# Down projection: each chunk begins with products of the first half of the tokens; layernorm's reciprocals written ahead of the gate evictions that follow

## Chip, cores, metric

One core of a Trainium2 chip runs the whole layer. The metric is the time of one execution on the device in microseconds (us), the median over runs of the same program. TensorE (PE) multiplies, VectorE (DVE) and ScalarE (ACT) do elementwise work and copy results out of PSUM, GpSimd (POOL) and SyncE (SP) here only issue transfers (DMA).

## The reference, cut to what matters

All tensors are float32; SEQ and D_MODEL are 1024, D_FF is 2816, D_CONF and D_SC 512, PLE_DIM 256, one layer.

```
h = rmsnorm(x, g_mix)
z = h @ w_in        # columns: conformer value | gate | shortconv B | C | V | merge gates A | B
a = a_val * sigmoid(a_gt)
a = causal_dwconv(a, conv_a_w) + conv_a_b                  # width 31
a = silu(layernorm(a, ln_a_g, ln_a_b))
y_a = a @ w_a_out
s = sc_b * causal_dwconv(sc_c * sc_v, conv_b_w)            # width 3
y_b = s @ w_b_out
x = x + (g_a * y_a + g_b * y_b) @ w_o
h = rmsnorm(x, g_ffn)
u = h @ w_up                                               # 1024 x 5632
f_gate = causal_dwconv(u[..., :D_FF], conv_f_w) + conv_f_b # width 3
f = gelu(f_gate) * u[..., D_FF:]
x = x + f @ w_down                                         # 2816 x 1024
x = x + sigmoid(rmsnorm(x, g_ple) @ w_ple_gate) * (p @ w_ple)
return rmsnorm(x, g_final)
```

## The kernel before, in words

Everything lies transposed: channels on the 128 partitions, the 1024 tokens along the free axis, in two halves H0 and H1 of 512 columns. One row is a tile of 128 channels x 1024 tokens. A float32 product is made of three products of rounded parts: each operand is cut into a hi (a cast on ScalarE, line 132) and a lo (a subtraction on VectorE, line 133), and hi by hi, lo by hi and hi by lo are added up in PSUM.

The input, up and down projections multiply two row blocks by two column blocks of weights with seven instead of eight products (Strassen in Winograd's form). The class Pair does one pair of output rows. Its method step(m) runs product m, of 3 matmuls for each input row pair: 1 and 2 multiply the two halves of the plain weights w_r by plain first-half columns of the rows, product 1 being copied to a second bank (line 639); 6 and 7 multiply sums of weights (s12 and s34, split into w_s_hi and w_s_lo) by sums of rows and go on in the copied bank, and after each of them the bank is copied out as u (lines 646 and 652); 5 is a sum by a sum too, 4 takes the plain weights w_q, 3 a sum of weights and plain columns. Its results go to four methods: use11 (after product 2), use21 (after 4), sum12 (after 3) and sum22 (after 5 and 7), the last two being the second half of the tokens. Of each pair of input rows four sums of quarters are needed (tiles t in the trace; fs is the split of those for products 5 and 7, ft of those for 6 and 4), and three plain quarters, f_q, for products 1, 2 and 3.

TensorE and SyncE work in the order in which the code is written. The order of ScalarE, VectorE and POOL is set by a scheduler while the program is built; tc.keep_in_program_order marks an instruction whose written place the scheduler is to keep against those written before it. On the chip each engine then works strictly along its own list, and an instruction that waits holds up all behind it.

The down projection takes its 22 rows of f, as 11 pairs, in three chunks of 4, 4 and 3 pairs (DROWS). Each chunk runs four pairs of output rows (p from 0 to 3) in the order that block_order makes: (0,1), (1,1), (0,2), (1,2), then (0,6), (0,5), (0,7) and so on, where (p, m) is product m of pair p. A product has 12 matmuls in the first two chunks and 9 in the last. Four products stand ahead of the first product 6. The rows of f were stored to HBM by the up projection; the class Rows loads them (load: two rows of 512 KB each), splits the plain quarters (plain) and makes and splits the sums (sums). Method prepare(ci, left) calls these by the products left in the work before. For the first chunk the rows are loaded six and three products before the up projection's end and the sums made at its last products; for the others loads stand 14 products ahead, plain splits 5, sums 2, 1 and 0.

In the first two chunks DnStore takes the results: it fills two tiles dn of 128x1024 and, once both halves are there, POOL adds each to x1 in HBM with an accumulating DMA of 512 KB (line 1152). In the last chunk DnLast loads the rows of x1 (both rows of the pair at its product 1), adds to them on VectorE (lines 1190 to 1201) and splits the result for the product with w_ple_gate. The class Loader fetches weights on SyncE's queue; the sums of weights are made by accumulating DMAs on POOL's queue (line 244).

The layernorm: ln_end runs between the products of s with w_b (gate evictions on line 922 are `gate = ps * gate`): variances by two small matmuls, sqrt on ScalarE, two reciprocals of 128x512 on VectorE (line 387, lrstd), then acc times lrstd (line 912), silu and the split to an_hi and an_lo, which TensorE needs for the products with w_a.

## Time and profile before

| what | value |
|---|---|
| runs shown: median (lowest, highest) | 1379.69 us (1376.6, 1381.29), 3 runs |
| profiled execution, its time | 1382.37 us |
| its span in the profile | 1380.6 us |
| TensorE busy | 1306.8 us (95%), 5798 matmuls |
| VectorE, ScalarE, POOL busy | 976.6 (71%), 590.3 (43%), 247.1 us (18%) |
| DMA | 245.25 MB, mean 178 GB/s |
| first matmul of the down projection's chunks | 1023.68, about 1117.6, about 1206.7 us |
| down projection ends | 1272.75 us |

The profile is of one execution, and its durations are read against its own span; the median of the runs is 2.7 us below this execution. Busy time of TensorE counts matmuls at half clock as busy too, so 95% doesn't mean that 5% is all that can be had. In a timeline a line says when an instruction began, how long it took and, in brackets, how long its engine had been idle and what ended that.

### The profile page before, as it was taken

The numbers are of one execution on the slowest core, as the hardware profiler recorded it, in microseconds if no ns is written. First come the engines' busy times: TensorE is split into PE (matmuls) and PEld (weight loads), VectorE is DVE, ScalarE is ACT, GpSimd is POOL, SyncE is SP. The second block draws the span as 40 slices with busy tenths as digits, with TensorE's granted clock in tenths as the row PEclk, the third lists the DMA queues.
The fourth block names the chain that finished last, engine by engine and source line by source line (L and its number), as shares of the span: only waits on it lengthen the run. The fifth ranks groups of instructions, "written<-read, shape, count | busy, mean of one in ns | idle before, by whom it ended". The sixth has DMA issues, their size and how long they took to land.

```text
span 1380.6 us, 15699 instructions
## 1 busy us (share of the span) xinstructions
PE 1306.8 (95%) x5798; PEld 1081.9 (78%) x5798; DVE 976.6 (71%) x1134; ACT 590.3 (43%) x814; POOL 247.1 (18%) x319
## 2 busy tenths in 40 slices
...
GB/s 339 183 119 125 179 237 159 142 200 212 196 272 233 122 24 130 163 205 189 177 167 175 198 186 172 174 168 192 187 181 162 272 222 204 211 234 153 76 91 73
DMA packets 102765, 245.25 MB, mean 178 GB/s; under 512 B 11680, under 2 KB 21664, under 8 KB 102688
## 3 DMA queue, kind: packets, MB, share of 16 engines
...
## 4 chain that ended last, share of the span: by engine, by line
PE 71%; DVE 14%; issue 8%; DMA 3%; ACT 2%; POOL 1%; SPq 0%; DVEq 0%; ACTq 0%; POOLq 0%
PE ps L629 50%; PE ps L155 14%; DVE acc L712 2%; PE ps L969 2%; PE ps L968 2%; PE ps L970 2%; DMA x_d<-dn 2%; DVE w_s_lo L133 1%; POOL s L244 1%; DMA f<-f_d 1%; DVE w_r_lo L133 1%; DVE x_raw L477 1%; DVE ft_lo L133 1%; DVE sc_cv L712 1%; DVE t L588 1%
## 5 line engine op out<-in xcount | busy, mean ns | idle before, releaser
L712 DVE SCALAR_TENSOR_TENSOR acc<-a,prm,acc 128x1023 f32<-128x1023 f32 (+14 forms) x120 | 151.8, 1265 | 1.7
L133 DVE TENSOR_TENSOR w_s_lo<-s,w_s_hi 128x1024 fp32r<-128x1024 f32 (+1 forms) x100 | 119.6, 1198 | 35.7 <-ACT w_s_hi L132 35.7
L244 POOL DMA_DIRECT2D s<-s x100 | 85.6, 856 | 298.2 <-DMA s<-s 126.0
L652 ACT COPY u<-ps 128x512 f32<-128x512 f32 x50 | 29.3, 586 | 202.3 <-PE ps L629 202.3
L132 ACT CAST w_s_hi<-s 128x1024 fp32r<-128x1024 f32 (+1 forms) x100 | 102.9, 1031 | 2.6 <-issue 1.7
L712 DVE SCALAR_TENSOR_TENSOR fg<-u_t,neg_f,fg 128x1023 f32<-128x1023 f32 (+1 forms) x44 | 56.5, 1283 | 28.3 <-ACT fg L706 27.6
L133 DVE TENSOR_TENSOR w_r_lo<-raw_r,w_r_hi 128x1024 fp32r<-128x1024 f32 (+1 forms) x50 | 59.8, 1197 | 17.2 <-ACT w_r_hi L132 17.2
L646 ACT COPY u<-ps 128x512 f32<-128x512 f32 x50 | 29.3, 586 | 92.4 <-PE ps L629 92.4
L629 PE MATMUL ps<-xgs_hi,w_s_lo 128*128 128x512 f32 x176 | 68.6, 390 | 0.0
L629 PE MATMUL ps<-xgs_lo,w_s_hi 128*128 128x512 f32 x176 | 68.5, 389 | 0.0
L629 PE MATMUL ps<-xgs_hi,w_s_hi 128*128 128x512 f32 x176 | 68.5, 389 | 0.0
L629 PE MATMUL ps<-xgp_hi,w_r_lo 128*128 128x512 f32 x176 | 68.5, 389 | 0.0
L629 PE MATMUL ps<-xgp_lo,w_r_hi 128*128 128x512 f32 x176 | 68.5, 389 | 0.0
L629 PE MATMUL ps<-xgp_hi,w_r_hi 128*128 128x512 f32 x176 | 68.5, 389 | 0.0
L639 ACT COPY ps<-ps 128x512 f32<-128x512 f32 x50 | 28.5, 571 | 87.6 <-PE ps L629 87.6
L1075 DVE TENSOR_TENSOR u_t<-ps,rstd 128x512 f32<-128x512 f32 x22 | 15.2, 691 | 69.7 <-PE ps L629 69.7
L155 PE MATMUL ps<-xp_hi,whi 128*128 128x448 f32 (+2 forms) x192 | 62.0, 323 | 1.9 <-DVE x L1201 1.9
L629 PE MATMUL ps<-xgq,w_s_hi 128*128 128x512 f32 x176 | 55.8, 399 | 7.2 <-DVE u_t L665 7.2
L155 PE MATMUL ps<-xp_lo,whi 128*128 128x448 f32 (+2 forms) x192 | 61.9, 323 | 0.0
L155 PE MATMUL ps<-xp_hi,wlo 128*128 128x448 f32 (+2 forms) x192 | 61.9, 323 | 0.0
L629 PE MATMUL ps<-xgt_hi,w_q 128*128 128x512 f32 x176 | 57.9, 390 | 0.7 <-ACT u L652 0.7
L629 PE MATMUL ps<-hss_hi,w_s_hi 128*128 128x512 f32 x128 | 50.9, 398 | 4.5 <-ACT w_s_hi L132 4.5
...
## 6 DMA issues: line engine op xcount, KB each, us to landing
s<-s POOLq DMA_DIRECT2D x92, 256.0 KB, 4.1
raw_r<-w_up SPq DMA_DIRECT2D x22, 512.0 KB, 4.7
s<-w_up SPq DMA_DIRECT2D x44, 256.0 KB, 3.0
s<-w_up SPq DMA_DIRECT2D x22, 512.0 KB, 5.8
s<-w_up POOLq DMA_DIRECT2D x44, 256.0 KB, 6.0
f_d<-v_t POOLq DMA_DIRECT2D x22, 512.0 KB, 5.9
f<-f_d SPq DMA_DIRECT2D x22, 512.0 KB, 9.8
s<-w_in SPq DMA_DIRECT2D x32, 256.0 KB, 3.2
```

The lines of the kernel that those rows point to most:

```text
L132: nc.scalar.copy(hi, src)
L133: nc.vector.tensor_sub(lo, src, f32(hi))
L155: nc.tensor.matmul(ps[:, :step], wt[:, b], xt[:, t : t + step], start=f, stop=l)
L244: nc.gpsimd.dma_start(dst, src, accum_op=ALU.add)
L629: nc.tensor.matmul(ps, wt[:, b], xt, start=f, stop=l, skip_group_check=True)
L639: nc.scalar.copy(self.b, self.a)
L646: nc.scalar.copy(self.e[:, H0], self.b)
L652: nc.scalar.copy(self.e[:, H1], self.b)
L712: nc.vector.scalar_tensor_tensor(dst[:, s:], src[:, : T - s], w(k), dst[:, s:], ALU.mult, ALU.add)
L968: nc.tensor.matmul(ps, whi[:, b], hi, start=first and k == ks[0], stop=False)
L969: nc.tensor.matmul(ps, whi[:, b], lo, start=False, stop=False)
L970: nc.tensor.matmul(ps, wlo[:, b], hi, start=False, stop=last and k == ks[-1])
```

## The change

In the down projection dn_order replaces block_order. In the first chunk all four products 1 come first, then all four products 2; in the other two they are interleaved as (0,1), (1,1), (0,2), (2,1), (1,2), (3,1), (2,2), (3,2). So eight products stand ahead of the first product 6, all of which need plain quarters of the first half of the tokens alone. In the rest of the chunk product 4 of a pair stands behind product 6 of the next. The last chunk ends with (3,4), (3,5), (3,3), where before it ended with (3,5), (3,4), (3,3).

Rows are loaded by halves: load0 the first-half tokens of a pair's two rows, load1 the second-half ones, as two DMAs of 256 KB each. The table STEPS gives, for the first chunk and for the others, the product at which each step of each pair of rows is written: negative numbers count back from the chunk's begin, positive ones from its first product. Sums are made in place and split in pairs (split23, split14). DnStore stores each half as soon as it is there: accumulating DMAs of 128x512, 256 KB, twice as many. DnLast loads the second row of its pair at product 6 and not at product 1.

In the layernorm, ln_end is cut in two. ln_stats has the variances, sqrt and reciprocals, and the first gate eviction of that round (first half) is marked to keep its written place, behind the reciprocals; the rest of ln_end is written behind the evictions of the round.

```diff
         return ap.bitcast(F32)
-    def halve(hi, lo, src):
-        nc.scalar.copy(hi, src)
+    def halve(hi, lo, src, pinned=False):
+        ins = nc.scalar.copy(hi, src)
+        if pinned:
+            tc.keep_in_program_order(ins)
         nc.vector.tensor_sub(lo, src, f32(hi))
...
         return order + [(n - 1, 4), (n - 1, 3)]
+    def dn_order(ci):
+        if ci == 0:
+            order = [(p, m) for m in (1, 2) for p in range(4)]
+        else:
+            order = [(0, 1), (1, 1), (0, 2), (2, 1), (1, 2), (3, 1), (2, 2), (3, 2)]
+        order += [(0, 6), (0, 5), (0, 7)]
+        for p in (1, 2):
+            order += [(p, 6), (p - 1, 4), (p, 5), (p - 1, 3), (p, 7)]
+        if ci < len(DROWS) - 1:
+            return order + [(3, 6), (2, 4), (2, 3), (3, 7), (3, 5), (3, 4), (3, 3)]
+        return order + [(3, 6), (2, 4), (3, 7), (2, 3), (3, 4), (3, 5), (3, 3)]
     def in_tiles(kind, i):
...
     ld.add_pairs("up", [(w_up[KF + j], w_up[j]) for j in range(KF)], up_order)
-    dn_order = block_order(KD // 2, 2)
     for ci, (k0, n) in enumerate(DROWS):
-        ld.add_pairs(("dn", ci), [(w_dn[j], w_dn[KD // 2 + j]) for j in range(KD // 2)], dn_order, k0, KH + k0, n)
+        pairs = [(w_dn[j], w_dn[KD // 2 + j]) for j in range(KD // 2)]
+        ld.add_pairs(("dn", ci), pairs, dn_order(ci), k0, KH + k0, n)
     for j in range(KD):
...
         an = []
-        def ln_end():
+        def ln_stats():
             for c in HALVES:
                 sqrt(lr[:, c], ps)
+            for c in HALVES:
                 inverse(lr[:, c])
+        def ln_end():
             for c in range(KC):
...
             gs.append(load_gates(KD, jj + 1) if jj < KC - 1 else load_gates(0, 0))
-            for j, g, pss in zip((jj, 4 + jj), gs[jj], half_products(s_t, ln_end if jj == 2 else None)):
+            for j, g, pss in zip((jj, 4 + jj), gs[jj], half_products(s_t, ln_stats if jj == 2 else None)):
                 for c, ps in zip(HALVES, pss):
-                    nc.vector.tensor_mul(g[:, c], ps, g[:, c])
+                    first = jj == 2 and j == jj and c is H0
+                    ins = nc.vector.tensor_mul(g[:, c], ps, g[:, c])
+                    if first:
+                        tc.keep_in_program_order(ins)
                 t_t[j] = g
+            if jj == 2:
+                ln_end()
             if jj == 0:
...
         class Rows:
+            STEPS = {
+                "load0": ((-8, -8, -8, -8), (-20, -19, -18, -17)),
+                "plain": ((-3, -3, -2, -2), (-12, -11, -10, -9)),
+                "load1": ((-2, -2, -2, -2), (-14, -13, -12, -11)),
+                "sums13": ((1, 1, 2, 2), (-8, -7, -6, -5)),
+                "sums24": ((2, 2, 3, 3), (-4, -3, -2, -1)),
+                "split23": ((3, 3, 4, 4), (0, 1, 2, 3)),
+                "split14": ((5, 5, 6, 6), (1, 2, 3, 4)),
+            }
             def __init__(self):
                 self.rows = [[{} for _ in range(n)] for _, n in DROWS]
-                self.raw = {}
-            def load(self, ci, i):
+                self.s0, self.s1 = {}, {}
+            def load(self, ci, i, c):
                 k = DROWS[ci][0] + i
-                self.raw[ci, i] = load(f_d[k], "f"), load(f_d[KH + k], "f")
+                t = slot("f")
+                nc.sync.dma_start(t[:, H0], f_d[k][:, c])
+                nc.sync.dma_start(t[:, H1], f_d[KH + k][:, c])
+                return t
+            def load0(self, ci, i):
+                self.s0[ci, i] = self.load(ci, i, H0)
+            def load1(self, ci, i):
+                self.s1[ci, i] = self.load(ci, i, H1)
             def plain(self, ci, i):
-                a, b = self.raw[ci, i]
+                t, r = self.s0[ci, i], self.rows[ci][i]
+                r[1], r[2] = half_split(t[:, H0], "f_1", True), half_split(t[:, H1], "f_2")
+            def sums13(self, ci, i):
+                t, v = self.s0[ci, i], self.s1[ci, i]
+                tc.keep_in_program_order(nc.vector.tensor_sub(t[:, H0], t[:, H0], v[:, H0]))
+                nc.vector.tensor_sub(v[:, H0], v[:, H1], v[:, H0])
+            def sums24(self, ci, i):
+                t, v = self.s0[ci, i], self.s1[ci, i]
+                self.rows[ci][i][3] = half_split(v[:, H1], "f_3")
+                nc.vector.scalar_tensor_tensor(v[:, H1], t[:, H0], -1.0, v[:, H1], ALU.mult, ALU.subtract)
+                nc.vector.scalar_tensor_tensor(t[:, H1], v[:, H1], -1.0, t[:, H1], ALU.mult, ALU.subtract)
+            def halves(self, ci, i, t, ma, mb):
+                hi, lo = split(t, "f_s")
                 r = self.rows[ci][i]
-                r[1], r[2] = half_split(a[:, H0], "f_q"), half_split(b[:, H0], "f_q")
-            def sums(self, ci, i):
-                a, b = self.raw[ci, i]
-                r = self.rows[ci][i]
-                r.update(sum_halves(*right_sums(a[:, H0], a[:, H1], b[:, H0], b[:, H1]), "f"))
-                r[3] = half_split(b[:, H1], "f_q")
-            def prepare(self, ci, left):
-                n = DROWS[ci][1]
-                if left == (6 if ci == 0 else 14):
-                    for i in range(2 if ci == 0 else n):
-                        self.load(ci, i)
-                if left == 5:
-                    for i in range(2 if ci == 0 else n):
-                        self.plain(ci, i)
-                if left == 3 and ci == 0:
-                    for i in range(2, n):
-                        self.load(ci, i)
-                        self.plain(ci, i)
-                if left == 2:
-                    self.sums(ci, 0)
-                if left == 1:
-                    self.sums(ci, 1)
-                if left == 0:
-                    for i in range(2, n):
-                        self.sums(ci, i)
+                r[ma], r[mb] = (hi[:, H0], lo[:, H0]), (hi[:, H1], lo[:, H1])
+            def split23(self, ci, i):
+                self.halves(ci, i, self.s1[ci, i], 7, 6)
+            def split14(self, ci, i):
+                self.halves(ci, i, self.s0[ci, i], 5, 4)
+            def prepare(self, ci, t):
+                if ci < len(DROWS):
+                    for step, at in self.STEPS.items():
+                        for i in range(DROWS[ci][1]):
+                            if at[min(ci, 1)][i] == t:
+                                getattr(self, step)(ci, i)
         f_rows = Rows()
...
             left = len(up_order) - 1 - n
-            f_rows.prepare(0, left)
+            f_rows.prepare(0, -left)
         rows = live = None
         class DnStore:
+            part = None
             def __init__(self, j):
-                self.j, self.o, self.n = j, (slot("dn"), slot("dn")), [0, 0]
-            def ready(self, i):
-                self.n[i] += 1
-                if self.n[i] == 2:
-                    nc.gpsimd.dma_start(x1_d[self.j + 4 * i], self.o[i], accum_op=ALU.add)
+                self.j = j
+            def out(self):
+                t = DnStore.part
+                DnStore.part = slot("dn") if t is None else None
+                return DnStore.part[:, H0] if t is None else t[:, H1]
+            def add(self, i, c, o):
+                nc.gpsimd.dma_start(x1_d[self.j + 4 * i][:, c], o, accum_op=ALU.add)
             def use11(self, ps):
-                nc.scalar.copy(self.o[0][:, H0], ps)
-                self.ready(0)
+                o = self.out()
+                nc.scalar.copy(o, ps)
+                self.add(0, H0, o)
...
             def sum22(self, c, e):
-                nc.vector.scalar_tensor_tensor(self.o[1][:, H1], c, -1.0, e, ALU.mult, ALU.subtract)
-                self.ready(1)
+                o = self.out()
+                nc.vector.scalar_tensor_tensor(o, c, -1.0, e, ALU.mult, ALU.subtract)
+                self.add(1, H1, o)
         x1, xg2 = [None] * KD, [None] * KD
...
                 self.j = j
-                for k in (j, j + 4):
-                    x1[k] = load(x1_d[k], "x2")
-                    xg2[k] = (slot("xp_hi", F32R), slot("xp_lo", F32R))
+                self.load(j)
+            def load(self, k):
+                x1[k] = load(x1_d[k], "x2")
+                xg2[k] = (slot("xp_hi", F32R), slot("xp_lo", F32R))
             def ready(self, k, c):
...
             live = {}
-            for n, (p, m) in enumerate(dn_order):
+            order = dn_order(ci)
+            for n, (p, m) in enumerate(order):
                 if m == 1:
                     live[p] = Pair(f_rows.rows[ci], (DnLast if last else DnStore)(p))
+                if m == 6 and last:
+                    live[p].to.load(p + 4)
                 live[p].step(m)
-                if not last:
-                    f_rows.prepare(ci + 1, len(dn_order) - 1 - n)
+                f_rows.prepare(ci, n + 1)
+                f_rows.prepare(ci + 1, n + 1 - len(order))
         live = None
```

VectorE at the end of the layernorm, where lrstd holds the reciprocals, gate_3088 and gate_3090 are the two tiles evicted in the round before or with them and gate_3154 the next; before:

```order
L922 TENSOR_TENSOR gate_3088<-ps_3164,gate_3088 128x512
L922 TENSOR_TENSOR gate_3088<-ps_3165,gate_3088 128x512
L133 TENSOR_TENSOR wlo_3095<-raw_2997,whi_3094 128x1024
L922 TENSOR_TENSOR gate_3090<-ps_3224,gate_3090 128x512
L922 TENSOR_TENSOR gate_3090<-ps_3225,gate_3090 128x512
L133 TENSOR_TENSOR wlo_3161<-raw_3092,whi_3160 128x1024
L387 RECIPROCAL lrstd_2992<-lrstd_2992 128x512 x2
L922 TENSOR_TENSOR gate_3154<-ps_3264,gate_3154 128x512
L912 TENSOR_TENSOR acc_2984<-acc_2984,lrstd_2992 128x1024
L912 TENSOR_TENSOR acc_2986<-acc_2986,lrstd_2992 128x1024
```

and now:

```order
L942 TENSOR_TENSOR gate_3088<-ps_3165,gate_3088 128x512
L135 TENSOR_TENSOR wlo_3095<-raw_2997,whi_3094 128x1024
L942 TENSOR_TENSOR gate_3090<-ps_3200,gate_3090 128x512
L942 TENSOR_TENSOR gate_3090<-ps_3201,gate_3090 128x512
L135 TENSOR_TENSOR wlo_3161<-raw_3092,whi_3160 128x1024
L403 RECIPROCAL lrstd_2992<-lrstd_2992 128x512 x2
L942 TENSOR_TENSOR gate_3088<-ps_3164,gate_3088 128x512
L931 TENSOR_TENSOR acc_2984<-acc_2984,lrstd_2992 128x1024
L931 TENSOR_TENSOR acc_2986<-acc_2986,lrstd_2992 128x1024
L931 TENSOR_TENSOR acc_2988<-acc_2988,lrstd_2992 128x1024
```

The first half of gate_3088 moved from ahead of the first wlo to behind the reciprocals, and gate_3154 from there to behind the four acc; both evictions of gate_3090 stay ahead of the reciprocals.

VectorE in the first chunk of the down projection, up to the split w_s_lo that its first product 6 needs (t, fs and ft are sums of rows and their parts; f_q and f_ with a number are plain quarters); before:

```order
L133 TENSOR_TENSOR fs_lo<-t_7337,fs_hi 128x1024
L133 TENSOR_TENSOR ft_lo<-t_7338,ft_hi 128x1024
L133 TENSOR_TENSOR f_q<-f,f_q 128x512
L586 TENSOR_TENSOR t_7354<-f 128x512
L587 TENSOR_TENSOR t_7354<-f 128x512
L588 SCALAR_TENSOR_TENSOR t_7355<-t_7354,f 128x512
L589 SCALAR_TENSOR_TENSOR t_7355<-t_7355,f 128x512
L133 TENSOR_TENSOR fs_lo<-t_7354,fs_hi 128x1024
L133 TENSOR_TENSOR ft_lo<-t_7355,ft_hi 128x1024
L133 TENSOR_TENSOR f_q<-f,f_q 128x512
L133 TENSOR_TENSOR w_s_lo<-s_7100,w_s_hi 128x1024
```

and now, where f<-f are the sums in place and f_s_lo their split:

```order
L1160 SCALAR_TENSOR_TENSOR f<-f 128x512
L135 TENSOR_TENSOR f_7386<-f,f_7386 128x512
L1161 SCALAR_TENSOR_TENSOR f<-f 128x512
L1160 SCALAR_TENSOR_TENSOR f<-f 128x512
L135 TENSOR_TENSOR f_7391<-f,f_7391 128x512
L1161 SCALAR_TENSOR_TENSOR f<-f 128x512
L1160 SCALAR_TENSOR_TENSOR f<-f 128x512
L135 TENSOR_TENSOR f_s_lo<-f,f_s_hi 128x1024
L1161 SCALAR_TENSOR_TENSOR f<-f 128x512
L135 TENSOR_TENSOR f_s_lo<-f,f_s_hi 128x1024 x5
L135 TENSOR_TENSOR w_s_lo<-s_7189,w_s_hi 128x1024
```

The splits of sums, before mixed in row by row, come together after all sums, and w_s_lo of the first pair stands behind six of them; the last two follow it.

VectorE in the last chunk, around the first splits of its weights (x are the rows of x1, xp_lo the split of a finished row, s_8356 to s_8418 before and s_8453 to s_8503 now the sums of weights); before:

```order
L1190 TENSOR_TENSOR x_8602<-ps,x_8602 128x512
L133 TENSOR_TENSOR w_s_lo<-s_8356,w_s_hi 128x768
L1190 TENSOR_TENSOR x_8629<-ps,x_8629 128x512
L133 TENSOR_TENSOR w_s_lo<-s_8357,w_s_hi 128x768
L1185 SCALAR_TENSOR_TENSOR xp_lo<-x_8602,prm,xp_hi 128x512
L133 TENSOR_TENSOR w_q<-raw_q,w_q 128x384
L1185 SCALAR_TENSOR_TENSOR xp_lo<-x_8629,prm,xp_hi 128x512
L426 TENSOR_TENSOR ssq<-ssq,sq 128x512
L133 TENSOR_TENSOR w_s_lo<-s_8418,w_s_hi 128x768
L1200 TENSOR_TENSOR x_8602<-x_8602,u_8700 128x512
```

and now:

```order
L135 TENSOR_TENSOR w_s_lo<-s_8453,w_s_hi 128x768
L1248 SCALAR_TENSOR_TENSOR xp_lo<-x_8630,prm,xp_hi 128x512
L442 TENSOR_TENSOR ssq<-ssq,sq 128x512
L1253 TENSOR_TENSOR x_8678<-ps,x_8678 128x512
L1253 TENSOR_TENSOR x_8713<-ps,x_8713 128x512
L135 TENSOR_TENSOR w_s_lo<-s_8454,w_s_hi 128x768
L1248 SCALAR_TENSOR_TENSOR xp_lo<-x_8678,prm,xp_hi 128x512
L442 TENSOR_TENSOR ssq<-ssq,sq 128x512
L135 TENSOR_TENSOR w_s_lo<-s_8503,w_s_hi 128x768
L1248 SCALAR_TENSOR_TENSOR xp_lo<-x_8713,prm,xp_hi 128x512
L442 TENSOR_TENSOR ssq<-ssq,sq 128x512
L135 TENSOR_TENSOR w_q<-raw_q,w_q 128x384
```

The adds onto x of all four pairs (L1190 before, L1253 now) now stand ahead of the second weight split, w_s_lo<-s_8454, where before two of them did.

## Rows read from the trace of the kernel before

**Rows 1.** Waits of TensorE, whole program: engine, line, releaser, us in total, times, longest.
```profile
PE ps L629 <- ACT w_s_hi L132: 28.9, 4, 12.0
PE ps L629 <- DVE u_t L665: 7.2, 1, 7.2
...
PE ps L629 <- ACT u L652: 2.7, 4, 0.7
...
PE ps L155 <- DVE x L1201: 1.9, 1, 1.9
...
PE ps L629 <- DVE w_r_lo L133: 0.7, 2, 0.5
```

**Rows 2.** Busy time by stretch: from:to, length, busy us per engine (instructions), clock, DMA share, GB/s.
```profile
1011.65:1272.75 261.10, 225.31 (x936) 180.96 (x936) 165.96 (x217) 125.98 (x183) 50.53 (x59) 0.93 0.79 200
1020.00:1047.45 27.45, 15.04 (x60) 11.64 (x58) 27.01 (x34) 15.57 (x19) 4.80 (x6) 0.81 0.51 127
1120.00:1144.53 24.53, 16.35 (x60) 12.49 (x59) 19.95 (x27) 13.86 (x18) 5.14 (x6) 0.79 0.97 242
1160.00:1180.00 20.00, 20.00 (x90) 16.57 (x89) 5.06 (x6) 6.39 (x9) 2.90 (x4) 1.00 1.00 267
```

**Rows 3.** Timeline of TensorE, down stretch: start, duration, engine, line, operation, [idle before <-releaser].
```profile
1018.82 1.22 PE L629 MATMUL ps<-xgq,w_s_hi 128*128 128x512 f32 x2 [7.17 <-DVE u_t L665]
...
1023.68 0.63 PE L629 MATMUL ps<-f_q,w_r_hi 128*128 128x512 f32 x2
...
1047.45 0.79 PE L629 MATMUL ps<-ft_hi,w_s_hi 128*128 128x512 f32 x1 [11.96 <-ACT w_s_hi L132]
...
1049.57 0.63 PE L629 MATMUL ps<-ft_hi,w_s_hi 128*128 128x512 f32 x1
1050.00 0.63 PE L629 MATMUL ps<-ft_lo,w_s_hi 128*128 128x512 f32 x1
...
1054.34 0.39 PE L629 MATMUL ps<-fs_hi,w_s_hi 128*128 128x512 f32 x1
...
1055.02 0.39 PE L629 MATMUL ps<-fs_hi,w_s_hi 128*128 128x512 f32 x1
...
1136.66 0.80 PE L629 MATMUL ps<-ft_hi,w_s_hi 128*128 128x512 f32 x1 [7.87 <-ACT w_s_hi L132]
...
1219.42 0.80 PE L629 MATMUL ps<-ft_hi,w_s_hi 128*128 128x512 f32 x1 [4.55 <-ACT w_s_hi L132]
...
1221.50 0.79 PE L629 MATMUL ps<-ft_hi,w_s_lo 128*128 128x512 f32 x1 [0.85 <-DVE w_s_lo L133]
```

**Rows 4.** Timelines of ScalarE and VectorE about the first chunk's begin.
```profile
1015.34 0.62 ACT L132 CAST f_q<-f 128x512 fp32r<-128x512 f32 x1 [1.87 <-DMA f<-f_d]
...
1024.87 1.25 ACT L706 ACTIVATE fg<-u_t,prm,neg_f 128x1024 f32<-128x1024 f32 x1
...
1046.35 1.04 ACT L132 CAST w_s_hi<-s 128x1024 fp32r<-128x1024 f32 x1
...
1018.08 0.68 DVE L665 TENSOR_TENSOR u_t<-ps,u 128x512 f32<-128x512 f32 x1
1018.68 0.68 DVE L586 TENSOR_TENSOR t<-f 128x512 f32<-128x512 f32 x1
...
1047.70 2.37 DVE L133 TENSOR_TENSOR w_s_lo<-s,w_s_hi 128x1024 fp32r<-128x1024 f32 x2
```

**Rows 5.** DMA issues (KB each, median us to landing), then the rows of tile x_d.
```profile
raw_r<-w_up SPq DMA_DIRECT2D x22, 512.0 KB, 4.7
s<-w_up SPq DMA_DIRECT2D x44, 256.0 KB, 3.0
...
f<-f_d SPq DMA_DIRECT2D x22, 512.0 KB, 9.8
...
L1152 POOL DMA_DIRECT2D x_d<-dn x16: 846/876/1537, 1063.9 to 1208.4; - x16
...
DMA to landing us min/median/max: 3.8/7.7/15.6
```

**Rows 6.** Timelines of VectorE and TensorE at the layernorm's end.
```profile
433.67 1.29 DVE L922 TENSOR_TENSOR gate<-ps,gate 128x512 f32<-128x512 f32 x2 [3.95 <-PE ps L155]
...
436.01 6.56 DVE L387 RECIPROCAL lrstd<-lrstd 128x512 f32<-128x512 f32 x2
...
447.64 0.73 PE L155 MATMUL ps<-an_hi,whi 128*128 128x512 f32 x2 [2.90 <-ACT an_hi L132]
450.63 1.22 PE L155 MATMUL ps<-an_lo,whi 128*128 128x512 f32 x2 [2.26 <-DVE an_lo L133]
```

14 lines of the change are left out of this document (8 added, 6 removed).

## The prediction

> **What bounds the kernel now.** I read the waits of the matmul engine first. TensorE is what the time goes by: in the 261.10 us from the last up product to the end of the down projection it runs 936 matmuls [rows 2]. At full clock one 128x512 matmul follows another after 0.227 us (three of them from 1054.34 to 1055.02) [rows 3], so 936 take 212.5 us. About 48.6 us of the stretch are lost. The waits by cause [rows 1] say where: weight halves w_s_hi that ScalarE casts (28.9 us in four waits, three of them here), the last state sum u_t (7.2, once), the copies u of line 652 (0.68 each), and x in the tail (1.9).
>
> The timeline of TensorE [rows 3] gives places and price. Each of the long stalls stands at the first use of something new at the begin of a chunk: 7.17 us before 1018.82, 11.96 before 1047.45, 7.87 before 1136.66, 4.55 before 1219.42. A stall costs more than its idle time: after 11.96 us of idleness the matmuls come at half rate (0.43 us, the 1.2 GHz level), and only at 1054.34 is the rate full. The next matmul was due at 1035.3; from there to 1054.34 are 19.0 us for 15 matmuls worth 3.4: 15.6 lost, 3.4 of it the clock and a small wait for w_s_lo. The 7.17 costs 9.5: 12 matmuls (2.7) due from 1011.5 would have made the chunk's first matmul come at 1014.2 and not at 1023.68. In the same way 7.87 costs 11.0 and 4.55 (with 0.85) 7.9. These four make 44.0 us of the 48.6; the rest are small waits.
>
> Why the operands are late: VectorE and ScalarE work in order. At 1015.34 ScalarE still casts a row of f that a transfer brought late [rows 4]; rows of f take 9.8 us to land [rows 5]. Behind it stand a weight's cast and split and then the sum of line 665 at 1018.08, for which TensorE waits. Then VectorE is busy for 27.01 of 27.45 us [rows 2] with sums and splits of all four rows of f, and the cast of w_s at 1046.35 and the split at 1047.70 come behind all of them [rows 4]. At the next chunk VectorE has 19.95 of 24.53 us [rows 2].
>
> **The down part, boundary of up and down.** Halves of the rows are now loaded eight products ahead instead of six or three, so the casts in front of the sum find their data: I place it at 1011.7, and TensorE is ready for it at 1011.5. Loss 0.45 in place of 9.5. The chunk then starts with four products 1. On ScalarE the cast of the second pair's weights stands behind a copy from PSUM, and those of the next two behind fg (1.25 us [rows 4]), another copy and gelu. Following that order by the rows' durations, product 1 of the second pair is ready 2.6 us late and the third and fourth together 1.05: 3.65 new. Call the end of the first pair's product E. Seven more products of 12 matmuls (2.72 each, 19.0) and 3.65 bring TensorE to product 6 at E+22.7. VectorE gets to the sums at E+9.4, when the last weights are split, and has 16 sums and 4 splits of 512 columns (0.60 each by the step from 1018.08 to 1018.68 [rows 4]), six splits of 1024 (1.19, half of the two at 1047.70 [rows 4]) and the split w_s_lo ahead of TensorE: 12.0 + 7.1 + 1.2 = 20.3. So w_s_lo is ready at E+29.6, TensorE idles about 6.5, and the clock takes 2.4 more (between 2.1 and 3.4, the price of the four stalls). That is 8.9 in place of 15.6. Before: 9.5 + 15.6 + 0.7 (w_r_lo) + 1.5 small ones = 27.3. After: 0.45 + 3.65 + 8.9 = 13.0 and some tenths. **Gain 13.8**, with 11.5 if the new waits of products 1 also slow the clock, 14.5 at best.
>
> **Next boundary.** Sums of the second chunk are made while the first still runs, one product ahead; after the begin only eight splits of 1024 columns (9.5 us), three weight splits (3.6) and w_s_lo (1.2) lie on VectorE against eight products (21.8 us). The whole 11.0 goes, with it 0.95 for a u copy (its product 4 no longer stands right behind product 7) and 0.35. **Gain 12.3**; a weight half has some 4 us of slack there, so it may be 9.
>
> **Third boundary.** By the same count 7.9 and 0.95 would go. But the last chunk adds its results onto rows of x1 that it loads, and for the fourth pair this load waits for the last stores of the chunk before. Two of these now stand on POOL's queue behind accumulations of new weights, which wait for landings. With T the begin of the chunk I place that store's issue at T+7 (an estimate: two landings of 3.0 [rows 5] and an issue), its landing 7.7 later (3.8 to 15.6 [rows 5]), the load 4.7 later [rows 5], so the add at T+19.5. Behind this add on VectorE stands the split of w_s34 of the first pair, and on ScalarE behind the cast of the added row the cast of w_s34 and a copy: some 4 to 8 us. Product 7 is due at T+20.4 (ten products of 2.04), so TensorE idles 3.3 to 7.3, with the clock about 7.5. The end of the last chunk gains 0.8 of the tail's wait and pays 0.9 for the sum of products 5 and 3 that now lie side by side. **Net gain 1**, from -4 (landing at 15.6) to +9 (no wait).
>
> **Stores.** 32 accumulating stores of 256 KB replace 16 of 512 KB. POOL pays 16 more issues of 0.88 [rows 5], 14 us over 260 in which it is a fifth busy: hidden. The same holds for SP's 22 more loads. The transfers are busy 0.79 of the stretch [rows 2], 206 us, to be done in 234: a share of 0.88, if halves cost half. There are rows on either side of this: 512 KB from SP land after 4.7 us and 256 KB after 3.0 [rows 5]. So the 38 additional transfers cost between nothing (latency alone, hidden by the earlier loads) and 1.3 each (twice 3.0 less 4.7), 49 us of engine time if it were all busy time. I take near nothing, since 7.7 us for a 512 KB store with a median twice that of a quarter-megabyte load looks like bytes; the other end is a rival.
>
> The Trainium skill speaks against halves: the page "SBUF — State Buffer", in "The DMA setup-cost knee", says that each transfer pays some fixed 2 us whatever its size, and that small ones never see the full rate. By its fit (an estimate from that page) two halves of 256 KB would take 2 us longer than one of 512 KB, 76 us for the 38 of them if nothing overlapped; the rows say 1.3 a pair.
>
> **The layernorm part.** TensorE waits 2.90 and 2.26 us for an_hi and an_lo [rows 6]. Both reciprocals (6.56 us from 436.01) run behind gate evictions that wait for TensorE until 433.67 [rows 6]. The words of the change promise them earlier. The built order does not: what goes behind the reciprocals is one eviction of an earlier gate, in place of a later one that stood there, while the two for which VectorE waits until 433.67 stay ahead. The products with acc start when they did; the moved eviction's bank is needed by nobody before. **Zero**, 0.3 either way.
>
> **Sum.** 13.8 + 12.3 + 1 + 0 = 27.1. From the profiled execution (1382.37 with what lies around its span of 1380.6) this gives 1355.3; from the median of the runs, 1379.69, it gives 1352.6. I say 1354. A measurement can tell 0.3%, 4 us, from no change.
>
> **Rivals.** First, **all boundaries clean**: the stores land quickly enough, no wait at the third begin, and the products 1 of the first chunk hide their weights better. Another 8 go: 1346. For it: 3.8 us is among the landings [rows 5]. Against it: the add needs store, load and add in a row. Chance 0.13.
>
> Second, **transfers become the bound**: 206 + 49 = 255 us of work would stand against 234; the share is already 1.00 from 1160 to 1180 [rows 2]. Then some 15 of the 27 are given back as late rows and weights: 1369. It is the page's rule as a mechanism of this kernel; the landings so far bear out a part of its price. Chance 0.2.
>
> Third, **slower than before**: POOL issues in order, and at each chunk's end up to eight half stores in a row, each waiting for its eviction, stand ahead of the accumulations of the next weights. Weights have some 4 us of slack; beyond that each us of delay is a us of TensorE at two boundaries, and 2.4 of clock each. To eat 27 us, each boundary must lose 13.5, so accumulations must come 4 + 11 = 15 us later than planned; landings over the median by 8 are the longest so far [rows 5]. At 18 later the sum is 27 - 2 x 16.4 = -6: 1386. Chance 0.03. Between it and the second case, no change that can be told: 0.04.
>
> Fourth, **the change doesn't do what it says**. For the layernorm that is my forecast. Should the reciprocals move to 429 after all, up to 5.2 idle and 2.6 of clock go: 1347. Chance 0.02, since the order is fixed in the program.
>
> **How the numbers follow.** The forecast has 0.58, between 1347 and 1362. The range of 8 in 10 takes in half of the first rival and the larger part of the second: 1344 to 1369. Faster 0.93 (forecast, first, second, fourth), same 0.04, slower 0.03.
>
> **What would show it.** Right: no wait for u_t at the end of up; short waits for w_r_hi and w_r_lo in the first products 1; a first wait for w_s of 6 to 7 us in the first chunk, none in the second, and one of 3 to 7 in the third for w_s34 or a u copy, with VectorE just before at an add that waited for a load of x; reciprocals still at 436. Wrong: waits at the second boundary (late weights, POOL behind its stores), landings of f or weights above 10 us and a transfer share near 1.0 for 100 us and more, or no wait at all in the third chunk.

## The result, and the profile after

| | before | changed |
|---|---|---|
| median of the runs (lowest, highest) | 1378.14 us (1376.37, 1381.29), 4 runs | 1356.1 us (1355.45, 1359.26), 4 runs |
| profiled execution | 1382.37 us, span 1380.6 | 1356.56 us, span 1354.8 |
| granted clock, mean of the span | 0.972 | 0.981 |
| first matmul of the down projection | at 1023.68 | at 1014.84 |
| first chunk | 94.07 us | 88.00 us |
| second chunk | 88.46 us | 76.16 us |
| third chunk, to the next projection's first matmul | 68.41 us | 70.00 us |

The ratio of the medians is 0.984 (95% interval 0.9816 to 0.9868): 22 us faster, inside the forecast range and 2 us above the forecast. Between the two profiled executions the difference is 25.8 us, and the table says where it comes from: 8.8 before the down projection's first matmul, 6.1 in the first chunk, 12.3 in the second, 1.6 given back in the third, and some 0.2 elsewhere.

First the waits of TensorE in the changed kernel, the same view as [rows 1] (engine, line, releaser, us in total, times, longest):

```profile
PE ps L645 <- ACT w_s_hi L132: 7.8, 2, 5.0
PE ps L645 <- DVE w_s_lo L135: 6.0, 4, 2.7
PE ps L645 <- ACT u L662: 5.4, 2, 4.1
...
PE ps L645 <- ACT ps L655: 2.0, 1, 2.0
...
PE ps L645 <- ACT w_r_hi L132: 1.6, 1, 1.6
...
PE ps L645 <- DVE w_r_lo L135: 1.2, 2, 0.7
```

The 28.9 us for w_s_hi have become 7.8, and only 2.85 of these are in the down projection. The 7.2 for u_t are gone. Among the new rows are ps of line 655, the copy of product 1 to its second bank, u of line 662, the copy after product 6 (once for 4.1), and w_r_hi, which product 1 needs. Then the stretches, as in [rows 2] (from:to, length, busy us of PE, PEld, DVE, ACT, POOL with instructions, clock, DMA share, GB/s): the whole down part and its three chunks.

```profile
1011.95:1249.00 237.05, 219.55 (x937) 177.76 (x937) 167.28 (x219) 122.15 (x182) 67.67 (x78) 0.97 0.91 227
1014.84:1102.84 88.00, 79.67 (x337) 63.79 (x336) 64.88 (x85) 45.36 (x65) 25.54 (x31) 0.96 0.96 237
1102.84:1179.00 76.16, 76.16 (x337) 63.06 (x336) 46.76 (x58) 37.17 (x54) 28.41 (x34) 1.00 1.01 240
1179.00:1249.00 70.00, 60.83 (x254) 48.55 (x252) 52.74 (x74) 39.45 (x63) 13.72 (x16) 0.95 0.74 193
```

In the second chunk TensorE is busy for all of 76.16 us at full clock: 336 matmuls at 0.227 us, nothing lost. That is so while the transfers' share reads 1.01. The first chunk loses 11.8 us, the third 12.9 (252 at 0.227 are 57.1).

TensorE's timeline shows the waits of the first chunk [rows 3 is the same view of before]:

```profile
1014.84 0.61 PE L645 MATMUL ps<-f,w_r_hi 128*128 128x512 f32 x2
...
1019.34 0.73 PE L645 MATMUL ps<-f,w_r_hi 128*128 128x512 f32 x2 [1.62 <-ACT w_r_hi L132]
1020.60 0.50 PE L645 MATMUL ps<-f,w_r_lo 128*128 128x512 f32 x1 [0.53 <-DVE w_r_lo L135]
1024.26 0.50 PE L645 MATMUL ps<-f,w_r_lo 128*128 128x512 f32 x1 [0.67 <-DVE w_r_lo L135]
1043.50 0.56 PE L645 MATMUL ps<-f_s_hi,w_s_hi 128*128 128x512 f32 x1 [2.85 <-ACT w_s_hi L132]
1047.16 0.79 PE L645 MATMUL ps<-f_s_hi,w_s_lo 128*128 128x512 f32 x1 [2.67 <-DVE w_s_lo L135]
```

No matmul waits at the first chunk's begin, none between 1047.16 and the third chunk. Of the third chunk's five waits the two large ones, read in the trace, stand at 1195.42 (1.98 for ps of line 655) and 1205.98 (4.14 for u of line 662), 16.4 and 27.0 us after its begin.

On VectorE the sum for which TensorE waited 7.17 us [rows 3, 4] now comes while TensorE is still at the products before it, and the first sum of the new chunk and the first w_s_lo stand where the prediction's count put them (1027.0 and 1047.2):

```profile
1011.21 0.68 DVE L681 TENSOR_TENSOR u_t<-ps,u 128x512 f32<-128x512 f32 x1
...
1027.03 0.69 DVE L1154 TENSOR_TENSOR f<-f 128x512 f32<-128x512 f32 x1
...
1045.88 1.22 DVE L135 TENSOR_TENSOR w_s_lo<-s,w_s_hi 128x1024 fp32r<-128x1024 f32 x1
```

What makes the third chunk wait is seen on four engines. POOL issues the last stores of the second chunk (line 1209) behind accumulations of weights (line 246). ScalarE, ahead of an activation into ssq, waits for a store's landing; ssq and dn are taken from the same pool of tiles, so that ssq gets the place of a dn tile is the likely reason. SyncE's load of x (line 872) waits for stores, and VectorE's add onto x waits for that load (the row that begins with SPq is from the view of waits, 1160 to 1215 us: total, times, longest):

```profile
1185.74 0.86 POOL L246 DMA_DIRECT2D s<-s  x1 [5.20 <-DMA x<-x_d]
...
1188.05 1.20 POOL L1209 DMA_DIRECT2D x_d<-dn  x1
1191.24 0.85 POOL L246 DMA_DIRECT2D s<-s  x1 [1.99 <-DMA s<-s]
1191.78 2.08 POOL L1209 DMA_DIRECT2D x_d<-dn  x2
...
1192.59 0.63 ACT L434 ACTIVATE ssq<-x 128x512 f32<-128x512 f32 x1 [4.02 <-DMA x_d<-dn]
...
1194.79 0.57 ACT L655 COPY ps<-ps 128x512 f32<-128x512 f32 x1
...
1203.80 0.72 ACT L1247 ACTIVATE xp_hi<-x,prm 128x512 fp32r<-128x512 f32 x1 [3.65 <-DVE x L1253]
...
1205.35 0.57 ACT L662 COPY u<-ps 128x512 f32<-128x512 f32 x1
...
SPq L872 <- DMA x_d<-dn: 22.7, 2, 17.3
...
1199.57 0.33 SPq L872 DMA_DIRECT2D x<-x_d  x1
...
1203.07 0.69 DVE L1253 TENSOR_TENSOR x<-ps,x 128x512 f32<-128x512 f32 x1 [4.93 <-DMA x<-x_d]
```

The copy at 1194.79 is released by nothing but ScalarE's own order: it stands behind the activation that waited 4.02 us. The same holds for the copy at 1205.35: ahead of it in ScalarE's list stands the cast of the added row, which waited 3.65 us for VectorE's add.

The layernorm has not moved. VectorE and TensorE there, to be read against [rows 6]:

```profile
436.22 6.56 DVE L403 RECIPROCAL lrstd<-lrstd 128x512 f32<-128x512 f32 x2
...
447.85 0.73 PE L157 MATMUL ps<-an_hi,whi 128*128 128x512 f32 x2 [2.90 <-ACT an_hi L132]
450.84 1.22 PE L157 MATMUL ps<-an_lo,whi 128*128 128x512 f32 x2 [2.26 <-DVE an_lo L135]
```

The DMA issues (KB each, median us to landing): first the stores of the kernel before, then two rows of the changed kernel. The 7.7 us in [rows 5] is the median of tile x_d, in which loads of x are counted with the stores; the stores alone took 8.5.

```profile
x_d<-dn POOLq DMA_DIRECT2D x16, 512.0 KB, 8.5
...
f<-f_d SPq DMA_DIRECT2D x44, 256.0 KB, 6.6
x_d<-dn POOLq DMA_DIRECT2D x32, 256.0 KB, 6.8
```

### The profile page after: what moved, and what is told of

It is laid out like the page before. It is cut to its first block, busy times and chain, and to the rows that moved or that the text cites. A ratio compares the mean times of both kernels' runs of the same rounds, so it can differ in the third digit from the quotient of the medians.

```text
span 1354.8 us, 15768 instructions
## 1 busy us (share of the span) xinstructions
PE 1300.3 (96%) x5798; PEld 1077.2 (80%) x5798; DVE 976.8 (72%) x1134; ACT 588.3 (43%) x814; POOL 261.7 (19%) x335
## 3 DMA queue, kind: packets, MB, share of 16 engines
q1 hardware_dynamic: 64800, 148.81, 33.2%
## 4 chain that ended last, share of the span: by engine, by line
PE 76%; DVE 13%; DMA 4%; issue 4%; ACT 3%; POOL 0%; SPq 0%; DVEq 0%; ACTq 0%; POOLq 0%
PE ps L645 54%; PE ps L157 14%; DVE acc L728 2%; PE ps L993 2%; PE ps L992 2%; PE ps L994 2%; DMA x_d<-dn 1%; DVE w_s_lo L135 1%; DMA s<-w_dn 1%; DMA x<-x_d 1%; DVE ssq L442 1%; DVE h_lo L498 1%; DVE sc_cv L728 1%; DVE w_r_lo L135 1%; DVE lrstd L403 0%
## 5 line engine op out<-in xcount | busy, mean ns | idle before, releaser
L645 PE MATMUL ps<-f_s_hi,w_s_hi 128*128 128x512 f32 x132 | 53.4, 404 | 8.2 <-ACT u L662 5.4
L645 PE MATMUL ps<-f,w_r_hi 128*128 128x512 f32 x176 | 54.5, 391 | 3.6 <-ACT ps L655 2.0
```

Of the source, the lines that this page charges most:

```text
L645: nc.tensor.matmul(ps, wt[:, b], xt, start=f, stop=l, skip_group_check=True)
```

## Experiments

Each ratio is against the kernel before in runs on the same chip, with its 95% interval. Lengths of chunks and waits come from the profiled execution of each kernel.

**The layernorm part alone**, put into the kernel before. Nothing else is changed.

> The kernel before with the layernorm part of the change alone. My theory: nothing, 1378 us within 2, and in the trace the two reciprocals again right behind the two gate evictions that wait for TensorE (6.56 us from about 436), the waits for an_hi and an_lo unchanged at 2.90 and 2.26 us. Rival (the pinned eviction is worth something, and the down part brought less than its trace says): 3 to 5 us faster, 1373 to 1375.

1381.16 us, ratio 1.0004 (0.999 to 1.0018). TensorE waits 2.90 and 2.26 us at the same matmuls, at 447.69 and 450.68. No gain can be told.

**The down part alone**: the changed kernel with the layernorm as before.

> The changed kernel with the layernorm part put back as it was before. My theory: the time of the changed kernel, 1356 us within 2, with the first chunk of the down projection 88.0 us long, the second 76.2 and the third 70.0. Rival (layernorm part has a share): 1359 to 1361.

1355.49 us, ratio 0.9818 (0.9804 to 0.9833); the chunks take 88.2, 76.2 and 73.1 us. The down part is the whole gain. The third chunk is the same code here as in the changed kernel, where it took 70.0; in the runs with the layernorm's line and with pinned copies below, which leave it alone too, it takes 72.9 and 72.7. So its length is known to some 3 us only.

**A layernorm part that does what the words say.** One line: all four evictions of the round keep their written place and not one.

```diff
-                    first = jj == 2 and j == jj and c is H0
+                    first = jj == 2
```

> The changed kernel with all four gate evictions of that round pinned, not the first alone, so that VectorE's list has the reciprocals ahead of the two evictions that wait for TensorE until 433.9. If it is these two that hold the reciprocals up, they begin at about 429.5, acc times lrstd 4.8 us earlier than 443.2 (four evictions of 0.60 now stand between), the wait for an_hi goes, that for an_lo falls to about 1.3 us, and with the half clock behind it 4 to 6.5 us go: 1350 to 1352. Rival (something else, the sqrt or the silu chain, sets the end): within 1 us of the changed kernel, 1356, with the waits unchanged.

1350.09 us (1346.14 to 1354.32), ratio 0.9783 (0.9755 to 0.981), the fastest kernel here. Its median is 5.4 us below that of the down part alone on the same chip; the two intervals touch, so the runs alone don't settle that it is faster, but the trace shows a gain of that size. VectorE and TensorE in it:

```profile
425.54 6.56 DVE L403 RECIPROCAL lrstd<-lrstd 128x512 f32<-128x512 f32 x2 [0.41 <-ACT lrstd L400]
432.02 2.42 DVE L942 TENSOR_TENSOR gate<-ps,gate 128x512 f32<-128x512 f32 x4
...
434.36 4.62 DVE L931 TENSOR_TENSOR acc<-acc,lrstd 128x1024 f32<-128x1024 f32 x4
...
443.26 0.72 PE L157 MATMUL ps<-an_lo,whi 128*128 128x512 f32 x2 [1.24 <-DVE an_lo L135]
```

The reciprocals run right behind the square roots, while TensorE makes the products whose evictions now stand behind them; the wait for an_hi is gone. The price of the two waits is seen in the same stretch of the two kernels, first of the down part alone, then of this one:

```profile
425.00:460.00 35.00, 29.84 (x118) 23.74 (x117) 25.84 (x24) 13.61 (x16) 0.00 (x0) 0.90 0.31 105
```

```profile
425.00:460.00 35.00, 33.68 (x148) 27.23 (x147) 29.31 (x30) 14.89 (x17) 0.00 (x0) 1.00 0.37 125
```

30 more matmuls fit into 35 us, 6.8 us at 0.227: 3.9 of it the idle time that is gone (2.90 and 2.26 less 1.24), the rest the clock, 1.00 in place of 0.90.

**The order of products alone**, put into the kernel before, with its loads, sums and stores.

> The kernel before with the new order of products alone: rows loaded whole and summed as before, stores of 512 KB as before, layernorm as before. My theory now (the order carries most, whole stores give back some 8 us, late rows keep the stall ahead of the first chunk): down part begins as late as before (7 to 9.5 us lost at the last sum of up), first chunk 83 to 88 us, the second 76 to 84, the third 68 to 74; in all 1360 to 1368. Rival (order, halves and early sums only work together): 1372 or more.

1382.54 us, ratio 1.0022 (1.001 to 1.0034); the chunks take 98.6, 89.8 and 73.3 us, each longer than before (94.07, 88.46, 68.41). I had expected a gain and missed. I had also expected the down part to begin as late as before, and it does not: its first matmul comes at 1014.27, and the wait for u_t is 2.27 us and not 7.17 (first row below), though the rows are loaded whole and at the same products as before. In the 33 us around the end of up (982 to 1015 here, 985 to 1018 before) POOL issues three transfers for sums of weights in place of seven, and the eight loads of rows land after at most 9.6 us and not 11.6; that this is the reason fits but wasn't tested. In the chunks the waits for w_s at the first product 6 are gone, and others for w_r have come, at products 1 of the later pairs (TensorE, then ScalarE's row that released the last of them):

```profile
1011.42 0.73 PE L642 MATMUL ps<-xgq,w_s_hi 128*128 128x512 f32 x2 [2.27 <-DVE u_t L678]
...
1028.76 1.22 PE L642 MATMUL ps<-f_q,w_r_hi 128*128 128x512 f32 x2 [4.97 <-ACT w_r_hi L132]
...
1132.38 1.22 PE L642 MATMUL ps<-f_q,w_r_hi 128*128 128x512 f32 x2 [11.15 <-ACT w_r_hi L132]
...
1128.49 1.04 ACT L132 CAST fs_hi<-t 128x1024 fp32r<-128x1024 f32 x1 [2.58 <-DVE t L600]
...
1131.29 1.99 ACT L132 CAST w_r_hi<-raw_r 128x1024 fp32r<-128x1024 f32 x2
```

With products 1 first, the weights of the second to fourth pair are needed before any sum, but their casts still stand behind the casts fs_hi and ft_hi of all rows, which wait for VectorE row by row. In the chunks the order moves the need, not the supply.

**The old order with everything else of the change** (block_order in all chunks, splits of the first chunk one product earlier, since they are needed earlier).

```diff
+        return block_order(KD // 2, 2)
...
-                "split14": ((5, 5, 6, 6), (1, 2, 3, 4)),
+                "split14": ((5, 5, 5, 5), (1, 2, 3, 4)),
```

> The changed kernel with the old order of products in all three chunks (four products ahead of the first product 6, not eight), while rows are loaded by halves and summed as early as now; the last splits of the first chunk are written one product earlier, since the old order needs them there. My theory (both are needed; the eight products give VectorE 10.9 us more, 8.2 in the last chunk): the first chunk waits about 10 us for w_s_lo in place of 5.5, since VectorE still has its 20 us of sums and splits, 7 to 10 us lost; the second waits some 0 to 4, since only 14 us of splits stand on VectorE against 10.9 us of products; in all 1364 to 1370. Rival (the early sums alone do it): 1354 to 1358. Rival (the order alone does it): back to 1372 to 1380.

1377.2 us, ratio 0.9978 (0.9965 to 0.9991): 3 us of the gain are left; the chunks take 98.4, 86.4 and 70.6 us. The time fits what was expected of a rival (the order alone does it), but the run above shows that the order alone makes nothing faster. So neither part has more than 3 us of its own in the whole time; the gain in the chunks comes only where both are. At the boundary each does most of it alone: the down part begins at 1012.34 here. In the first chunk, beside 1.62 and 0.53 for w_r, the waits are for f_s_hi and f_s_lo (3.83, 4.68, 0.62, 1.62, 0.47): four products do not cover the sums. In the second chunk:

```profile
1119.43 0.80 PE L635 MATMUL ps<-f,w_r_hi 128*128 128x512 f32 x1 [5.78 <-ACT w_r_hi L132]
...
1118.33 1.04 ACT L132 CAST w_r_hi<-raw_r 128x1024 fp32r<-128x1024 f32 x1 [14.42 <-issue]
```

ScalarE stands idle for 14.42 us ahead of this cast, and the trace names nothing that released it. I can't say what it waited for.

**Sums later**: in the second and third chunk at the places of the kernel before (two, one and no products ahead, the splits of products 6 and 7 at the chunk's begin and behind its first product), all else as changed.

```diff
-                "sums13": ((1, 1, 2, 2), (-8, -7, -6, -5)),
-                "sums24": ((2, 2, 3, 3), (-4, -3, -2, -1)),
-                "split23": ((3, 3, 4, 4), (0, 1, 2, 3)),
+                "sums13": ((1, 1, 2, 2), (-2, -1, 0, 0)),
+                "sums24": ((2, 2, 3, 3), (-2, -1, 0, 0)),
+                "split23": ((3, 3, 4, 4), (0, 0, 1, 1)),
```

> The changed kernel with the sums for the second and third chunk written at the last three products of the chunk before, as the kernel before had them, and not four to eight products ahead; eight products still stand ahead of the first product 6. My theory: VectorE has 20 us of sums and splits from about five us ahead of the chunk's begin, against 21.8 us of products in the second chunk and 16.3 in the third, so no wait or up to 3 us in the second, 2 to 6 in the third: 1356 to 1362. Rival (the early sums are what took the second boundary's stall away): 7 us and more lost at the second boundary, 1363 or more.

1355.64 us, ratio 0.9821 (0.9799 to 0.9842): no difference that can be told. Inside there are two that cancel: the second chunk takes 81.97 us (5.8 more, with a wait of 3.76 for a w_r_lo at 1111.78), the third 65.21 (4.8 less, the 4.14 for u is 2.02 and the 1.98 for the copy is gone). So the sums' early place is what makes the second chunk clean. The third is shorter here than in any other run, but it also follows a second chunk that took 5.8 us longer; which of the two does it isn't separated.

**Stores of whole rows**: DnStore as before, 16 accumulating DMAs of 512 KB.

```diff
+            def ready(self, i):
+                self.n[i] += 1
+                if self.n[i] == 2:
+                    nc.gpsimd.dma_start(x1_d[self.j + 4 * i], self.o[i], accum_op=ALU.add)
...
-                self.add(0, H0, o)
+                self.ready(0)
```

> The changed kernel with the results of the first two chunks stored as before, 16 accumulating DMAs of 512 KB in place of 32 of 256 KB. My theory: the transfers' share in the down stretch falls from 0.91 to 0.88 or 0.89 and nobody gains by it, since no engine waits for bandwidth; the stores of a chunk's last pair start as late as now and land later, so the third begin loses up to 3 us more: 1356 to 1359. Rival (halves are dear, 1.3 us of engine time each): the share falls below 0.85 and 3 to 6 us go, 1350 to 1353.

1363.76 us, ratio 0.9879 (0.9856 to 0.9902). By the ratios this is 5 us over the changed kernel (the intervals touch) and 8 over the down part alone (they don't), more than I had expected. The transfers' share falls, from 0.96 and 1.01 in the first two chunks to 0.86 and 0.94, and yet the second chunk takes 83.74 us against 76.16. The third takes 72.26, no more than the same code took with half stores (70.0 to 73.1), so the loss is the second chunk's. ScalarE and TensorE where it loses, then the long wait of the third chunk on TensorE and VectorE:

```profile
1108.97 1.04 ACT L132 CAST w_r_hi<-raw_r 128x1024 fp32r<-128x1024 f32 x1 [6.56 <-DMA x_d<-dn]
...
1111.49 1.22 PE L645 MATMUL ps<-f,w_r_hi 128*128 128x512 f32 x2 [4.58 <-ACT ps L655]
...
1214.06 0.80 PE L645 MATMUL ps<-f_s_hi,w_s_hi 128*128 128x512 f32 x1 [8.20 <-ACT u L662]
...
1211.16 0.69 DVE L1243 TENSOR_TENSOR x<-ps,x 128x512 f32<-128x512 f32 x1 [4.81 <-DMA x<-x_d]
```

The idle time of ScalarE ends with the landing of a store, and what stands behind it is a copy from PSUM for which TensorE waits. That a row which is stored when both its halves are there leaves its tile later fits this wait. It isn't shown apart from the size: the edit brings back larger transfers, and also two tiles that a pair keeps from its product 1 on. Half stores with their use of tiles are not a burden that happens to be hidden; they carry a part of the gain.

**Copies of product 1 pinned** on ScalarE in the first chunk, ahead of the casts and fg of later pairs.

```diff
-                    nc.scalar.copy(self.b, self.a)
+                    ins = nc.scalar.copy(self.b, self.a)
+                    if pinned:
+                        tc.keep_in_program_order(ins)
```

> The changed kernel with the copies of product 1 in the first chunk pinned on ScalarE behind what is written ahead of them, so that the casts of the second to fourth pair's weights don't stand behind them. If that order on ScalarE is the cause of the waits of 1.62, 0.53 and 0.67 us in the first products, they shrink to 1 us together, the sums on VectorE begin some 3.5 us earlier, and w_s_lo of the first product 6 with them: first chunk 84 to 85 us in place of 88.0, 1351 to 1353. Rival (the weights themselves land late): the waits stay, 1356.

1352.53 us (1349.18 to 1355.71), ratio 0.98 (0.9774 to 0.9826). The interval touches that of the changed kernel, so the whole time doesn't settle it; the chunk does: 84.63 us in place of 88.00. The waits of 1.62 and 0.53 us are gone and those for w_s_hi and w_s_lo are 2.43 and 2.44. The chunk's idle time is 2.9 us less, 2.15 of it these two waits, and the chunk is 3.4 shorter. In the whole execution most of this is lost again: the third chunk takes 72.7 us, with waits of 3.71 and 3.10.

**Product 2 of the fourth pair later** in the last chunk, behind (0,7), so that its add stands behind the first pair's splits.

```diff
+        late = ci == len(DROWS) - 1
+        if late:
+            order.remove((3, 2))
...
+        if late:
+            order.append((3, 2))
```

> The changed kernel with product 2 of the fourth pair in the last chunk moved from ahead of the first product 6 to behind product 7 of the first pair, so that the add onto the row of x1 that is loaded last stands later on VectorE. If store, load and add hold up the copies and splits behind them, the wait of 4.14 us for a copy u at product 7 goes with some 2 us of half clock; the wait of 1.98 us at a product 2 of that chunk stays, since it comes from ScalarE's waiting for another store. 1350 to 1353 us, last chunk 64 to 66 us in place of 70.0. Rival (late weights are the cause, the add only stands in front of them): the wait moves to a weight half w_s of the same product, last chunk 69 to 70, 1356.

1359.14 us, ratio 0.9849 (0.9834 to 0.9864): not better, and the third chunk takes 75.3 us. The 4.14 us for u at product 7 are gone, the 1.98 for the copy too, and a new wait stands at the chunk's begin (TensorE, then VectorE):

```profile
1185.62 0.80 PE L650 MATMUL ps<-f,w_r_lo 128*128 128x512 f32 x1 [6.16 <-DVE w_r_lo L135]
...
1184.61 0.96 DVE L135 TENSOR_TENSOR w_r_lo<-raw_r,w_r_hi 128x768 fp32r<-128x768 f32 x1 [11.38 <-issue]
```

VectorE idles for 11.38 us ahead of the split. The last stores go out at 1183.65, 1191.11 and 1194.61, again behind accumulations of weights; that this split's tile came free with one of those landings fits but isn't shown.

**The adds of product 2 deferred**: in the last chunk what follows product 2 (the fourth pair's add, and the splits and squares of all pairs' first halves) is written behind (0,7), the add pinned there.

```diff
-                x = x1[self.j][:, H0]
-                nc.vector.tensor_add(x, ps, x)
+                self.ps = ps
+                if self.j < 3:
+                    x = x1[self.j][:, H0]
+                    nc.vector.tensor_add(x, ps, x)
...
+                if last and (p, m) == (0, 7):
+                    for q in range(4):
+                        live[q].to.late(q == 3)
```

> The changed kernel with the work on the results of product 2 in the last chunk written later, behind product 7 of the first pair: the splits and squares of the four first results, and for the fourth pair also the add onto the row of x1, which is pinned there. The order on TensorE is the same. If the add's wait for store and load, and the wait of a square for a slot, are what hold up ScalarE and VectorE ahead of products 2 and 7, then the waits of 1.98 to 3.7 us and of 3.1 to 4.2 us in the last chunk go and with them 2 to 4 us of half clock: last chunk 61 to 64 us in place of 70.0, 1347 to 1351. Rival (slots of the weight halves wait for the same landings): a wait of 2 to 4 us stays at product 7, now for a w_s, last chunk 65 to 67.

1364.63 us, ratio 0.9886 (0.986 to 0.9912), far from what I expected. The first waits did go: TensorE runs the eight products of the begin without one. Then the pile that was moved is in the way (VectorE, then ScalarE, then TensorE):

```profile
1210.73 0.69 DVE L1276 TENSOR_TENSOR x<-x,u 128x512 f32<-128x512 f32 x1 [9.94 <-DMA x<-x_d]
...
1212.30 0.72 ACT L1247 ACTIVATE xp_hi<-x,prm 128x512 fp32r<-128x512 f32 x1 [10.86 <-DVE x L1277]
...
1221.84 0.57 ACT L662 COPY u<-ps 128x512 f32<-128x512 f32 x1
...
1212.27 1.22 PE L645 MATMUL ps<-f,w_s_hi 128*128 128x512 f32 x2 [5.31 <-DVE x L1277]
...
1222.47 0.79 PE L645 MATMUL ps<-f_s_hi,w_s_hi 128*128 128x512 f32 x1 [5.99 <-ACT u L662]
```

The next load of x, of a second row, is waited for on VectorE for 9.94 us, and behind it ScalarE has activations from 1212.30 on ahead of the copy at 1221.84. The chunk takes 82.2 us.

**Three edits together** (the layernorm's line, the pinned copies, the deferred adds), and then the same with the sums of the last chunk at their late places.

> The changed kernel with three edits together: all four gate evictions pinned, copies of product 1 in the first chunk pinned, the deferred work of the last chunk. If the three act at different places and add up: 5.4 + 3 + 6 us less than 1356, so 1340 to 1344. Rival (what is gained early only lets later stores and loads collide): 1347 to 1350.

> The three edits together, and the last chunk's sums made at the end of the chunk before as in the kernel before (the second chunk's stay early). In the run with late sums the last chunk took 65.2 us in place of 70.0. If that came from shorter waits behind loads and slots, which the deferred work already removes: the same as without, 1340 to 1344. Rival (it came from rows that keep their slots for a shorter time): 1 to 3 us less.

1357.29 us, ratio 0.9821 (0.9795 to 0.9847), and 1355.26, ratio 0.9818 (0.9801 to 0.9834). Both keep the first two gains (the first chunk takes 84.6 us in the first of them) and lose them in the third chunk, 82.05 and 79.3 us, with waits of 5.99 and 6.96 for a copy u. The layernorm's line with the pinned copies and without the deferred adds was not run.

## Why the prediction was right, point by point

**The boundary of up and down**: forecast 9.05 gained (9.5 less 0.45), measured 8.8. The sum of line 681 runs from 1011.21 to 1011.89, where I had placed it at 1011.7, and the products behind it begin at 1011.95, 0.3 us later than they could. The size is right, but the cause that I named, halves loaded earlier, is not needed for most of it: with the order alone, the loads whole and at the old products, the wait is 2.27 us. The order also sets which weights are fetched ahead of the chunk, which I had left out.

**The first chunk**: forecast 12.6 lost (3.65 and 8.9), measured 11.8. The count of VectorE's work was right to a tenth: with E, the end of the first pair's product 1, at 1017.6 the sums begin at 1027.03 (E + 9.4) and w_s_lo is there at 1047.1 (forecast E + 29.6, 1047.2). Two sizes inside were off a little, against each other. The waits of products 1 came where they were named, 2.15 us at the second pair (forecast 2.6) and 0.67 at the third (1.05 for the third and fourth), and cost 3.9 with the clock. The wait for w_s is not one of 6.5 but 2.85 for the hi part and 2.67 for the lo part, 5.5, and costs 7.9 and not 8.9: from 1040.5, when product 6 was due, to 1050.69, when the rate is full again, are 10.2 us for 10 matmuls. The run with pinned copies shows the place named on ScalarE to be the cause of the waits at the second pair.

**The second chunk**: forecast 12.3 gained, measured 12.3. Of the 4 us of slack that I gave the weights nothing was needed.

**The third chunk**: forecast a net gain of 1, measured 1.6 lost, inside the bounds of -4 and +9; in the down part alone the same code lost 4.7, just outside them. The mechanism was the one named: stores behind accumulations, the load of x behind them, VectorE's add waiting, a copy u waiting on ScalarE behind the added row. The wait of 4.14 us lies in the 3.3 to 7.3 forecast. The term that was mis-sized is the store's issue: T + 7 in the prediction, T + 9 and T + 12.8 in the trace (T, the chunk's begin, is 1179.0), since the first accumulation waited 5.20 us for a landing (the trace names that of a load of x) and the next two followed one by one. The load went out at T + 20.6 and the add came at T + 24.1, not T + 19.5; it did not cost more because product 7, due at T + 20.4 in the prediction, was itself due only at T + 22.8 (1205.98 less 4.14). That lateness is the step that was missing: the activation into ssq waits 4.02 us for a store's landing and holds the copy of line 655, a wait of 1.98 us on TensorE. That the two errors nearly cancel is luck. The bounds themselves rest on a misread row: 3.8 to 15.6 counts loads of x with the stores, and stores alone took 5.8 to 15.6, so the 3.8 that was held for the first rival was no store.

**The stores**: I priced 32 half stores as work that is hidden, with a bound of 1.3 us for each of 38 additional transfers. Over the down part the transfers were busy 0.79 of 261.10 us before, 206.3, and 0.91 of 237.05 now, 215.7: 9.4 us more, 0.25 for each. The stretch also moved 1.6 MB more (227 GB/s over 237.05 us against 200 over 261.10), so not all of this need be the halves'; over the whole program the shares of the two large queues (32.6 and 32.1% of 1380.6 us, then 33.2 and 33.0% of 1354.8) differ by some 4 us. The second rival (transfers become the bound) falls with it: the share stands at 1.01 for a whole chunk in which TensorE loses nothing. But the reason that I gave for the low price, that landings look like bytes, is wrong: half a store lands after 6.8 us, a whole one after 8.5 before and 7.2 in the run with whole stores. The time in the engines was nearly the same in all, so it about halves with the size; the time to landing does not. And what I had not counted at all is the other side: storing by halves is worth 5 to 8 us by the run with whole stores, in the second chunk, which I took to be clean either way. That it is worth this because half rows leave their tiles earlier is likely, not shown.

The Trainium skill's rule against halves (page "SBUF — State Buffer", section "The DMA setup-cost knee": a fixed 2 us or so in each transfer) would make 76 us for the 38 if nothing overlapped, an estimate worked out from that page. The same section of the Trainium skill says that most of the 2 us is the wait until a landing is confirmed. The trace agrees with that reading: halves land nearly as late as wholes, and the 38 additional transfers show as some 9 us of engine time or less, not 76.

**The order**: the prediction spoke of one change with parts that add up. They don't. The order alone makes it 3 us slower, the rest without it 3 faster, both together (the down part alone) 25 faster. What the loads by halves, the early sums and the later load of x are worth one by one was not run. The prediction's steps were right for the whole; anyone who had taken "eight products in place of four cover the sums" as the cause would have been wrong, as I was in the expectation for the order alone.

**The layernorm**: forecast zero, measured 1.0004. The reason given, two evictions that stay ahead of the reciprocals, is shown by the run that pins all four: then the reciprocals move to 425.54 and the gain is the one of the fourth rival (5.2 idle and 2.6 of clock there, 3.9 idle and some 3 of clock here).

What stays open: in the last chunk both edits aimed at its waits (product 2 later, the adds deferred) removed them and met longer ones elsewhere, 75.3 and 82.2 us for the chunk; the late sums, not aimed at it, left the shortest, 65.2; and the unchanged code took 70.0 to 73.1. Waits for landings of stores or loads are seen in those that I read, but which tile's release decides in which variant I haven't settled.
